# Attention over sequences of varied length: V projected by tiles of 512 columns, two runs of scores for two tiles, direct jumps between loop bodies

## Chip, cores, metric

One core of one Trainium2 chip. The metric is the device time of one execution in microseconds. Verdicts rest on ratios, which use fast runs alone; medians and ranges are of all runs of a kernel (among them one slow run each of e4, of e11 and of the kernel before). In the profile PE is TensorE, PEld its weight loads, DVE VectorE, ACT ScalarE, POOL GpSimd, SP SyncE; PEclk is the TensorE clock that was granted, in tenths of full speed (in the table by windows as a fraction).

## The reference

```python
# x: 32 x 512 x 512 fp32, w_qkv: 512 x 1536, lengths: 32 integers from 64 to 511, 8 heads of 64
for b in range(32):
    n = lengths[b]
    q, k, v = np.split(x[b, :n] @ w_qkv, 3, axis=-1)       # by heads: 8 x n x 64
    attn = softmax(q @ k.T / 8)
    output[b, :n] = attn @ v                                # the rows behind n stay zero
```

The lengths are data: the kernel sorts the sequences on the chip and picks the code for each pair at run time.

## The kernel before

The 32 sequences, sorted by length, form 16 pairs. A pair belongs to a *class* `k`, which computes N = 512 - 32k columns in T = ceil(N/128) tiles. Each class is one unrolled *body* with two halves. A half does the scores, exponentials and products of one sequence and projects Q, K and V of the next. For this input the pairs have the classes 0, 2, 4, 5, 5, 5, 6, 7, 8, 9, 9, 10, 11, 11, 12, 13. So there are two bodies of four tiles, six of three, six of two and two of one. Between bodies there are two steps by two classes (0 to 2 and 2 to 4), nine steps by one, and four repeats of the same class.

A half is a string of tokens, in the order of TensorE's work: `S` one run of scores with its exponential on ScalarE, `Q0`, `K0` a projection (*evicted*, that is copied out of the matmul's output bank, by VectorE, by ScalarE when lower case), `B0`/`b0` Q and K of a head pair together, `V0` a V group, `A0` attention times V with its normalization (`R`, `X` are its two VectorE parts when placed by hand), `O`, `P` the stores.

```python
    ORDER = {
        4: "S S Q0 A0 S S K0 V0 S S Q1 A1 S S K1 V1 S S Q2 A2 S S K2 V2 S S Q3 A3 S S K3 V3 O",
        3: "S S Q0 A0 K0 S S V0 Q1 A1 S S K1 V1 S S Q2 A2 K2 S S V2 Q3 A3 S S K3 V3 O",
        2: "S S V0 B0 A0 b1 A1 S V1 S B2 V2 O A2 A3 b3 P V3",
    }

    def vproj(pr, bank, h, i, T):          # the V of head pair i, for all T tiles
        ...                                # (T == 1: one group of 512 columns)
        for t in range(T):
            for c in range(NC):            # NC = 4
                mms.append(mm(pa[:, bank, t * P : (t + 1) * P],
                              xT[h][:, c, t * P : (t + 1) * P],            # stationary
                              w_r[:, c, 2 * D + i * P : 2 * D + (i + 1) * P],  # 128 moving columns
                              c == 0, c == NC - 1))
        group(... "dve" ... tensor_tensor(out=v_aug[...], in0=pa[...], in1=mask, op=ALU.mult))
```

The walk through the bodies is the same on every engine. The program stands in the order of the classes, and each body has a compare-and-branch at its head (skip it unless the class is this one) and one at its end (repeat it if the next pair has the same class). TensorE alone also gets a hint, some way into the first half, for the head branch of the next class (a mark ahead of a branch, tied to that branch, with a register as its condition):

```python
    def read_class(pr, h, N):              # after the third projection of the first half
        ...
                def hint(e):
                    cur, far = regs[e.engine][1], regs["far"]
                    e.reg_alu(far, cur, k + 2, ALU.is_lt)       # 1: class k+1 will not be skipped
                    ahead[k + 1] = e.mark_branch_hint_location(far)
                pr.add("pe", hint)

    def loops(e, name, body, pre1=None):
        r, cur = regs[e.engine]
        for k, N in enumerate(CLASSES):
            ...
            br = e.br_cmp(cur, k, lab, out_, "IS_EQ")           # else to out_, the head of k+1
            if name == "pe" and k in ahead:
                br.branch_hint(ahead[k])
            nc.switch_bb(lab, parent=top)
            body(e, N)
            e.br_cmp(cur, k, lab, out_, "IS_EQ")                # repeat
            nc.switch_bb(out_, parent=top)
```

The softmax here doesn't subtract the row's maximum and nothing guards it: scores larger than these inputs give would overflow.

## Time and profile before

| | before |
|---|---|
| time, median of four fast runs (range), those of the rounds with the kernel after | 369.78 us (368.31 to 371.26) |
| profiled span, mean granted clock | 367.7 us, 0.986 |
| TensorE busy | 349.1 us, 95% |
| start of the loop's first projection | 30.72 us |
| a half of four tiles, 512 columns | 19.50 us |
| two halves of three tiles, 352 columns | 25.6 us for both |

TensorE, busy 95% of the span, is the bound, so a change is read off the starts of its groups. Two further lines matter later. The first is the row of the granted clock in 40 slices of the span, the second the only entry for a pause without a visible cause ("issue") among TensorE's waits (columns: in total, times, longest).

```profile
PEclk9699999999999999999999999999999999999998
```

```profile
PE pa L219 <- issue: 0.4, 1, 0.4
```

Behind the start-up the clock drops only in the last slice, and no "issue" pause is longer than 0.4 us. That one stands at 109.69, inside a body, so none falls on the fifteen steps between bodies. (In the one-tile part, waits of up to 1.2 us are put down to TensorE's own sequencer, in the helper that waits for semaphores; their cause is not shown.)

### The profile page before, as it was taken

How to read it: one execution, taken by the hardware profiler on the slowest of the kernel's cores; microseconds unless marked ns; L12 is line 12 of the kernel's file. 1: busy time of each engine (PE TensorE's matmuls, PEld its weight loads, DVE VectorE, ACT ScalarE, POOL GpSimd, SP SyncE). 2: the span in 40 equal slices, each digit the busy share in tenths (PEclk: the TensorE clock that was granted, in tenths of full speed). 3: DMA queues.
4: the chain of work that ended last, by engine and by line, in shares of the span. 5: the costliest groups of instructions: out<-in, count | busy, mean ns of one | idle time of the engine just before them, and what ended most of it. 6: DMA issues, size and time to landing. Idle time of an engine off the chain costs nothing. (4 is left out here: it accounts for less than half of the span.)

```text
span 367.7 us, 12708 instructions
## 1 busy us (share of the span) xinstructions
PE 349.1 (95%) x4844; PEld 245.4 (67%) x4845; DVE 236.9 (64%) x537; ACT 229.2 (62%) x307; POOL 58.0 (16%) x85
## 2 busy tenths in 40 slices
PE   8699999999999999999999999999899999999882
PEld 3245566666656666666666677777789898887761
DVE  4455667666767667676766767676666666676562
ACT  5278778777776666666666757565566664654541
POOL 3062020202010110111011001110112112212120
PEclk9699999999999999999999999999999999999998
DMA  7969677458759677978759759969876566667673
GB/s 264 337 155 276 202 160 215 132 123 265 182 168 237 172 257 192 225 260 289 225 150 302 252 117 286 299 199 255 233 203 184 152 176 182 188 143 223 164 169 101
DMA packets 84582, 76.43 MB, mean 208 GB/s; under 512 B 42544, under 2 KB 63024, under 8 KB 84528
## 3 DMA queue, kind: packets, MB, share of 16 engines
q1 hardware_dynamic: 69376, 59.47, 59.8%
q10 hardware_dynamic: 15152, 16.26, 12.9%
q8 instruction: 32, 0.52, 0.6%
q14 instruction: 22, 0.18, 0.2%
HBM read 29.37 MB, written 36.70 MB: 180 GB/s over the span
## 5 line engine op out<-in xcount | busy, mean ns | idle before, releaser
L261 ACT ACTIVATE ep<-psc 128x704 f16<-128x704 f32 (+5 forms) x265 | 204.7, 821 | 101.3 <-PE psc L219 76.6
L219 PE MATMUL pa<-xT,w_r 128*128 128x352 f16 (+11 forms) x1056 | 161.6, 288 | 3.8 <-PEq L45 2.6
L291 DVE CAST qkT<-pa 128x352 f16<-128x352 f32 (+5 forms) x164 | 92.0, 561 | 59.5 <-PE pa L219 55.5
L219 PEld LDWEIGHTS pa<-xT,w_r 128*128 128x128 f16 x1056 | 81.4, 98 | 54.4 <-issue 27.9
L219 PE MATMUL pa<-w_r,xT 128*128 128x128 f16 (+1 forms) x1296 | 94.8, 221 | 0.1
L219 PEld LDWEIGHTS pa<-w_r,xT 128*128 128x128 f16 x1296 | 77.8, 98 | 18.4 <-issue 9.4
L324 DVE TENSOR_TENSOR v_aug<-pa,masks 128x384 f16<-128x384 f32 (+2 forms) x116 | 60.9, 525 | 31.5 <-PE pa L219 29.7
L219 PEld LDWEIGHTS pav<-v_aug,ep 128*128 128x128 f16 x1792 | 67.2, 98 | 11.7 <-ACT ep L261 3.5
L219 PE MATMUL pav<-v_aug,ep 128*128 128x65 f16 x1792 | 71.7, 194 | 2.5 <-ACT ep L261 2.4
L219 PE MATMUL psc<-qkT 64*128 64x352 f16 (+11 forms) x656 | 70.1, 299 | 1.4 <-PEq L45 0.9
L405 DVE SCALAR_TENSOR_TENSOR onat<-pav,masks,rcp 128x256 f32<-128x256 f32 (+2 forms) x128 | 51.9, 444 | 5.2 <-DVE rcp L381 0.7
L849 POOL CAST v_aug<-masks 128x24 f16 (+4 forms) x33 | 9.1, 276 | 282.1 <-POOLq L665 282.1
L844 POOL CAST x<-x_nat 128x1536 f16<-128x1536 f32 (+3 forms) x34 | 43.9, 1293 | 17.2 <-POOLq L665 16.2
L219 PEld LDWEIGHTS psc<-qkT 64*128 64x128 f16 x656 | 20.6, 94 | 21.5 <-issue 10.2
L289 ACT CAST qkT<-pa 128x448 f16<-128x448 f32 (+3 forms) x28 | 14.1, 504 | 24.4 <-ACTq L45 15.2
L381 DVE RECIPROCAL rcp<-pav 128x8 f32<-128x8 f32 (+1 forms) x68 | 14.7, 216 | 19.7 <-PE pav L219 16.0
L403 DVE TENSOR_TENSOR onat<-pav,rcp 128x512 f32<-128x512 f32 (+2 forms) x32 | 17.8, 557 | 1.1
L883 PE MATMUL psc<-zt 128*128 128x512 f16 x26 | 7.9, 468 | 1.7 <-DVE zt L905 1.7
L883 PEld LDWEIGHTS psc<-zt 128*128 128x128 f16 x26 | 2.8, 114 | 5.2 <-issue 1.9
L610 ACT ACTIVATE ep<-tiny 128x1024 f32<-128x1024 f32 x6 | 6.0, 1053 | 0.0
L790 ACT CAST w_r<-w_f 128x1024 f16<-128x1024 f32 x4 | 4.2, 1045 | 1.1 <-DMA w_f<-in_w_qkv_dram 1.1
L790 ACT ACT_TABLE_LOAD x1 | 1.3, 1283 | 3.2 <-issue 3.2
(48 smaller groups left out, 19.7 us busy)
## 6 DMA issues: line engine op xcount, KB each, us to landing
out_dram<-zt SPq DMA_DIRECT2D x16, 768.0 KB, 5.4
x_nat<-in_x_dram SPq DMA_DIRECT2D x12, 768.0 KB, 5.0
x_nat<-in_x_dram SPq DMA_DIRECT2D x8, 1024.0 KB, 6.6
out_dram<-onat ACTq DMA_DIRECT2D x28, 256.0 KB, 3.5
x_nat<-in_x_dram SPq DMA_DIRECT2D x12, 512.0 KB, 4.2
out_dram<-onat ACTq DMA_DIRECT2D x12, 384.0 KB, 3.9
out_dram<-onat SPq DMA_DIRECT2D x12, 384.0 KB, 3.6
out_dram<-zt SPq DMA_DIRECT2D x12, 256.0 KB, 4.6
```

The source lines that it names most:

```text
L219: return lambda e: e.matmul(o, lhsT, rhs, start=start, stop=stop)
L261: lambda e: e.activation(out=dst, in_=src, func=AF.Exp, scale=scale),
L289: group(pr, b, eng, mms, lambda e: e.copy(out=dst, in_=src))
L291: group(pr, b, eng, mms, lambda e: e.tensor_copy(out=dst, in_=src))
L324: lambda e: e.tensor_tensor(out=v_aug[h][:, 0:T, 2 * i : 2 * i + 2, 0:HD], in0=pa[:, bank, 0 : T * P].rearrange("p (t a d) -> p t a d", a= ...
L381: pr.add("dve", lambda e: e.reciprocal(out=rv, in_=den).then_inc(s_r, 1))
L403: ins = e.tensor_tensor(op=ALU.mult, **ops)
L405: ins = e.scalar_tensor_tensor(scalar=now[0][:, 1, t : t + 1], op0=ALU.mult, op1=ALU.mult, **ops)
L610: lambda e, a=a: e.activation(out=ep32[:, i + 1, a], func=AF.Copy, in_=tiny.unsqueeze(2).broadcast_to([P, NT, MAXS // 2]),).then_inc(s_ini ...
L844: e.tensor_copy(out=x16[h][:, 0:T, :], in_=x_nat[h][:, 0:T, :]).then_inc(s_xc[h], 1)
L849: e.tensor_copy(out=v_aug[h][:, 0:T, :, HD], in_=src[:, 0, 0:T].unsqueeze(2).broadcast_to([P, T, NH]),).then_inc(s_on[h], 1)
L883: e.matmul(psc[:, 1, 0, :], zt16[:, 0:P], zt16[:, 0:MAXS], start=True, stop=True)
```

## The change

It has four parts.

1. V by tiles for T = 3 and 4 and in the prologue (T = 1 had it already): the x tile stands still, all 512 V columns move, one group for each tile. T = 2 keeps the old form under the name `W`.
2. New orders: two runs of eight score matmuls for T = 2 instead of one of eight and two of four; some K and Q copies moved to ScalarE; V3 ahead of the last products, Q3 last.
3. Jumps: the end of a body compares the next class with its own, the next and the next but one, and jumps there directly.
4. Hints: TensorE, ScalarE and VectorE each get a hint for the jump to the body after next, and none for the next. The prologue and the bodies of classes 0 to 9 and 12 carry one; those of 10, 11 and 13 have no such jump.

The diff, cut to its core (cut: renamed variables, the halves rewritten for bodies of mixed classes, which `DOWN = 0` leaves unused, and a class table for 32 lengths):

```diff
-    def vproj(pr, bank, h, i, T):
+    def vproj(pr, bank, h, t):
+        mms = []
+        for c in range(NC):
+            mms.append(
+                mm(pa[:, bank, :], xT[h][:, c, t * P : (t + 1) * P], w_r[:, c, 2 * D : 3 * D],
+                   c == 0, c == NC - 1)
             )
+        group(
+            pr, f"a{bank}", "dve", mms,
+            lambda e: e.tensor_scalar(
+                out=v_aug[h][:, t, :, 0:HD],
+                in0=pa[:, bank].rearrange("p (h d) -> p h d", d=HD),
+                scalar1=now[0][:, 0, t : t + 1], scalar2=None, op0=ALU.mult,
+            ),
+        )
...
     ORDER = {
-        4: "S S Q0 A0 S S K0 V0 S S Q1 A1 S S K1 V1 S S Q2 A2 S S K2 V2 S S Q3 A3 S S K3 V3 O",
-        3: "S S Q0 A0 K0 S S V0 Q1 A1 S S K1 V1 S S Q2 A2 K2 S S V2 Q3 A3 S S K3 V3 O",
-        2: "S S V0 B0 A0 b1 A1 S V1 S B2 V2 O A2 A3 b3 P V3",
+        4: "S S Q0 A0 S S V0 k0 S S q1 A1 S S K1 V1 S S Q2 A2 R2 X2 S S K2 V2 S S V3 A3 O S S K3 Q3",
+        3: "S S k0 A0 Q0 S S V0 q1 A1 S S K1 V1 S S q2 A2 S S K2 V2 A3 R3 X3 S S K3 O Q3",
+        2: "S S W0 A0 B0 b1 A1 W1 S S B2 W2 A2 A3 R3 X3 O W3 P B3",
+        1: "Q k A0 V0 S O",
     }
...
-                def hint(e):
-                    cur, far = regs[e.engine][1], regs["far"]
-                    e.reg_alu(far, cur, k + 2, ALU.is_lt)
-                    ahead[k + 1] = e.mark_branch_hint_location(far)
+    def fetch(pr, at, to):                 # called with to = at + 2, after the fourth projection
+        if to not in targets(at) or to <= at + 1:
+            return
+        def fn(g, e):
+            e.reg_alu(regs[g], regs[e.engine][1], number(to), ALU.is_equal)
+            pr.ahead[g][to] = e.mark_branch_hint_location(regs[g])
+        for g in ("pe", "act", "dve"):
+            pr.add(g, lambda e, g=g: fn(g, e))
...
+        def leave(at, ahead):
+            for to in targets(at):         # itself, at + 1, at + 2
+                d = f"{name}_d{at}_{to}"
+                br = e.br_cmp(cur, number(to), f"{name}_b{to}", d, "IS_EQ")
+                if to in ahead:
+                    br.branch_hint(ahead[to])
+                nc.switch_bb(d, parent=top)
+            e.br(f"{name}_x{max(targets(at))}")
...
-            body(e, N)
-            e.br_cmp(cur, k, lab, out_, "IS_EQ")
+            leave(at, body(e, at) or {})
```

## The prediction

> **What bounds the kernel now.** I read the page's busy shares first, then the matmul timeline from start to start (recorded ends overlap the next start), then waits, then VectorE and ScalarE where TensorE waits.
>
> ```profile
> PE 349.1 (95%) x4844; PEld 245.4 (67%) x4845; DVE 236.9 (64%) x537; ACT 229.2 (62%) x307; POOL 58.0 (16%) x85
> ```
>
> TensorE is busy 95% of 367.7 us; no other engine is near. Of the missing 18.6 us most lies in the first 14 us and after 345 us. So what counts is the time from one group's start to the next group's start. Two pieces of its timeline, of a four-tile and a three-tile body (V is `pa<-w_r,xT`, Q and K are `pa<-xT,w_r`, scores `psc`):
>
> ```profile
> 32.67 0.61 PE L219 MATMUL psc<-qkT 64*128 64x512 f16 x4
> 33.21 1.04 PE L219 MATMUL pa<-xT,w_r 128*128 128x512 f16 x4
> 34.08 1.06 PE L219 MATMUL pa<-w_r,xT 128*128 128x128 f16 x16
> 35.07 0.61 PE L219 MATMUL psc<-qkT 64*128 64x512 f16 x4
> ...
> 115.66 0.84 PE L219 MATMUL pa<-w_r,xT 128*128 128x128 f16 x12
> 116.34 0.81 PE L219 MATMUL pa<-xT,w_r 128*128 128x384 f16 x4
> ```
>
> Four matmuls of 512 columns take 34.08 - 33.21 = 0.87 us, 0.2175 each. Twelve of 128 columns take 116.34 - 115.66 = 0.68, 0.0567 each. Sixteen take 0.99 where scores follow, of which 16 x 0.0567 = 0.91 is work and 0.08 is the step into the scores.
>
> The two-tile body, where runs of scores are of eight or four matmuls:
>
> ```profile
> 324.93 0.45 PE L219 MATMUL psc<-qkT 64*128 64x160 f16 x8
> 325.31 0.62 PE L219 MATMUL pa<-w_r,xT 128*128 128x128 f16 x8
> 325.77 0.72 PE L219 MATMUL pa<-xT,w_r 128*128 128x160 f16 x8
> ...
> 327.47 0.31 PE L219 MATMUL psc<-qkT 64*128 64x160 f16 x4
> 327.71 0.62 PE L219 MATMUL pa<-w_r,xT 128*128 128x128 f16 x8
> 328.26 0.31 PE L219 MATMUL psc<-qkT 64*128 64x160 f16 x4
> ```
>
> Eight together take 0.38; two fours take 2 x 0.24 or 0.25 = 0.49. The V group ahead takes 0.46 when a projection follows and 0.55 when scores follow. A run less saves 0.11 + 0.09 = 0.20 us.
>
> The waits of TensorE between 30 and 346 us, then the place where one arises, at the end of a three-tile body's second half (VectorE, then TensorE):
>
> ```profile
> PE pav L219 <- ACT ep L261: 2.4, 3, 1.1
> PEld pa L219 <- DVE qkT L291: 6.7, 22, 0.4
> ```
>
> ```profile
> 156.85 0.23 DVE L381 RECIPROCAL rcp<-pav 128x12 f32<-128x12 f32 x1
> 157.23 1.27 DVE L405 SCALAR_TENSOR_TENSOR onat<-pav,masks,rcp 128x256 f32<-128x256 f32 x3
> 158.41 0.51 DVE L291 CAST qkT<-pa 128x352 f16<-128x352 f32 x1
> ```
>
> ```profile
> 158.41 0.47 PE L219 MATMUL psc<-qkT 64*128 64x352 f16 x4
> 158.99 0.77 PE L219 MATMUL pa<-xT,w_r 128*128 128x352 f16 x4
> ```
>
> From the scores to the next projection are 0.58 us instead of the usual 0.40: the bank frees only when VectorE, after the A3 products, has copied K3 (158.92). Most of the 6.7 us of weight-load idle is ordinary lead; what TensorE really loses in the three-tile bodies is about 0.05 to 0.27 us at such places.
>
> [...]The trace shows no such gap on TensorE at the jump from class 0 to 2 (scores at 69.19, projection at 69.68: 0.49, as elsewhere in that body). [...]I take the 0.20 us from the trace.
>
> **The change, part by part.** The sixteen bodies, from the lengths: two of four tiles, six of three, six of two, two of one; each has two halves. `DOWN` is 0, so both halves keep one size and the "shorter" orders are never used.
>
> *V by tiles.* Four tiles: 4 groups of 0.907 become 4 of 0.870, 0.15 us a half, 4 halves: 0.6 us. Three tiles: 4 x 0.68 = 2.72 becomes 3 x 0.87 = 2.61, 0.11 a half, 12 halves: 1.4 us. The runs of scores stay eight and six. The eviction becomes tensor_scalar; the one-tile body has it at 749 ns for 128x512, against 4 x 558 or 4 x 694 now, so VectorE gains in three tiles and pays 0.2 us in four.
>
> *The prologue* also gets 512-column V, but its scores wait for ScalarE, which from 20.92 to 30.34 us does exponentials and memory fills without a gap. Nothing is gained. The class table doubles (32 x 15) and needs two more VectorE steps: about 1.2 us on VectorE before 10 us, mostly hidden by the input that lands at 11.84. Cost 0.2 us.
>
> *Evictions on ScalarE* (k0, q1, and q2 in three tiles). In four tiles ScalarE has 1.94 of each 2.4 us taken and gets two copies of 0.59 a half. By hand its lag grows to 0.5 us, just short of the slot that the next scores want. I count no wait.
>
> *Three-tile end of a half.* K3 is still copied after V2 and the A3 products, and k0 wants its bank. From A3's end to the wanted start: scores 0.41, K3 0.61, Q3 0.69, scores 0.41: 2.12 us (V3 gave 0.76 in place of 0.69). The products now also start behind the wider V2 eviction, about 0.1 later, so the bank is free at about 2.5 in a second half and 2.1 in a first. Waits of 0.25 to 0.6 instead of 0.12 to 0.27 at seconds, and 0 to 0.27 at firsts for the short classes: 1.5 us more over the bodies. The waits before q2 (about 0.5 us in all) go. Net cost 1.0 us; three tiles net -0.4 us.
>
> *Two tiles.* One run less: 12 x 0.20 = 2.4 us. But W3 moves ahead of B3, and its eviction waits behind A3's products. From A3's end (330.13) these are done at 331.69, W3 would be copied at 332.02: 1.9 us. W0 wants the bank after 0.46 + 0.64 + 0.38 = 1.48 at 160 columns, 1.8 at 224. That costs 0.2 to 0.5 us where columns are few, 0.8 in sum. Two body starts gain nothing, as ScalarE sets them (below): 0.4. The bridge to one tile waits for all banks, and its last one now frees 0.5 us later. Net -0.7 us.
>
> *Jumps.* An own or next class needs the same one or two compares as before; only a jump by two gets a new hint on ScalarE and VectorE, and this input has two such, both without a gap on TensorE. ScalarE does start late after a body, as here:
>
> ```profile
> 331.91 0.39 ACTq L673 DMA_DIRECT2D out_dram<-onat  x1
> 333.74 1.30 ACT L261 ACTIVATE ep<-psc 128x640 f16<-128x640 f32 x2 [2.34 <-issue]
> ```
>
> The 1.44 us from the end of the store's issue to the exponential cause one of the three waits of TensorE for `ep` (0.90 at 334.50). But this is a repeat of the same class, without a hint in either kernel. I count 0, give or take 1 us.
>
> Sum: +0.2 - 0.6 - 0.4 - 0.7 = -1.5 us, 367.9. The hand count charges every wait in full, and orders this particular look tried out; I shade to 367.6.
>
> **Rivals.** (1) All gain, no new wait: 0.6 + 1.4 + 2.4 us, and the present bank and ScalarE waits vanish too (about 3 us): 362 us. For it: the copies moved to ScalarE relieve VectorE. Against: K3 and W3 are still behind the products. (2) ScalarE becomes the bound in the four-tile bodies: 18 operations of 0.92 to 1.02 and 0.59 in 19.3 us is 91%; if the lag does not recover within a half, each of four halves loses up to 1 us: 371 us. Against: the run is 1.94 of 2.4 and 1.73 of 2.2 at 448. (3) Jumps stall VectorE, ScalarE or the DMA queue (now a taken jump, where the next body was run into): 0.5 us at fifteen bodies would be 375 us; the queues' idle time hides most of it. (4) The stretch before the two-tile bodies waits for zero stores (ScalarE 3.28 us at 257.9): a faster start only lengthens that wait.
>
> **Range.** All gain without waits gives 362, twice my waits 371. Range 363.8 to 371.0. Faster by over 2% needs less than 362.0, beyond the whole gain: 0.05. Slower by over 2% needs stalls at every body end: 0.04. Within: 0.91.
>
> **What would show it.** V groups of 16 and 12 matmuls at 0.87 to four, and halves of four tiles 0.15 us shorter; no gain before the loop. In three tiles, scores at a half's start followed by k0 after 0.6 to 0.8 us with a wait for VectorE; in two tiles, two score runs a half and a wait ahead of W0 in the 160-column bodies; the bridge's idle of 0.86 at 1.3. I am wrong if those waits are absent (then 364 to 365), if ScalarE delays scores in four tiles, or if gaps with the sequencer as releaser stand at body ends.

The sum: +0.2 (start) - 0.6 (four tiles) - 0.4 (three tiles) - 0.7 (two tiles) = -1.5 us, and 0 for the jumps. In rival (3), the 0.5 us a body is a supposition from no trace, and that idle time hides most of it was the author's estimate (the page before leaves VectorE idle for 36% and ScalarE for 38% of the span), which the result did not bear out.

## The result and the profile after

| | before | after |
|---|---|---|
| median of four fast runs (range) | 369.78 us (368.31 to 371.26) | 396.32 us (393.34 to 397.11) |
| profiled span, clock | 367.7 us, 0.986 | 395.3 us, 0.956 |

The ratio is 1.070 (95% interval 1.063 to 1.078): the change makes the kernel 7% slower. (A ratio here and below is the mean time of one kernel's fast runs over that of the other's fast runs of the same rounds, so not quite the ratio of the medians.)

The page of the kernel after, busy shares and granted clock:

```profile
PE 355.8 (90%) x4172; PEld 220.9 (56%) x4173; DVE 221.8 (56%) x495; ACT 239.5 (61%) x339; POOL 58.5 (15%) x85
```

```profile
PEclk9699999999989989999999899999999999979995
```

TensorE has 672 matmuls less, yet is busy 6.7 us longer, over a span 27.6 us longer. The clock row says why it is busy longer: it now has dips in the middle of the run. And TensorE's waits say where the rest is (columns as before):

```profile
PE pav L228 <- issue: 6.3, 3, 2.8
PE pa L228 <- issue: 5.4, 3, 3.0
PE pa L228 <- DVE v_aug L335: 4.1, 3, 3.6
PE psc L228 <- issue: 3.5, 2, 1.9
```

"issue" is 6.3 + 5.4 + 3.5 = 15.2 us in eight pauses, where it was 0.4 us in one. The engine waited for nothing that the profile shows. To find where, set the start of each body's first scores beside the same start before. The lag (after minus before) rises at some steps and not at others:

| body of class | 0 | 2 | 4 | 5 | 5 again | 5 again | 6 | 7 | 8 | 9 | 11 | 11 again | end |
|---|---|---|---|---|---|---|---|---|---|---|---|---|---|
| lag at its first scores, us | 0.1 | 1.6 | 4.5 | 5.4 | 9.7 | 9.8 | 9.8 | 14.3 | 14.5 | 16.7 | 17.9 | 23.9 | 27.6 |

(For class 0 it is taken at the first projection, 30.85 against 30.72, as the scores ahead of it are split in one of the two.) A pause falls before a body's first scores or up to 8 us behind them, and then shows at the next entry: the 4.3 us between 5 and its repeat belong to the step from 4 to 5, the 4.5 between 6 and 7 to the step from 5 to 6. The repeats of class 5 themselves cost next to nothing (the lag goes from 9.7 to 9.8 us). TensorE's timeline at the step from class 4 to class 5 (start, duration, group; in brackets the idle time before it and what ended it):

```profile
141.97 0.76 PE L228 MATMUL pa<-xT,w_r 128*128 128x352 f16 x4
142.57 0.28 PE L228 MATMUL pav<-v_aug,ep 128*128 128x65 f16 x4
145.44 0.92 PE L228 MATMUL pav<-v_aug,ep 128*128 128x65 f16 x14 [2.58 <-issue]
...
146.99 1.35 PE L228 MATMUL pa<-xT,w_r 128*128 128x352 f16 x4
```

A run of 18 products is cut after four, stands for 2.58 us, and goes on. Nothing in the program separates the fourth product from the fifth. In the kernel before, the same products in the same body are one run:

```profile
136.86 0.71 PE L219 MATMUL pav<-v_aug,ep 128*128 128x65 f16 x18
137.51 0.47 PE L219 MATMUL psc<-qkT 64*128 64x352 f16 x4
```

And the price goes on afterwards: the projection of four matmuls takes 0.60 us from start to start at 141.97 and 148.13 - 146.99 = 1.14 us behind the pause. The same place by windows (window, its length, busy us and instructions of PE, PEld, DVE, ACT, POOL, then granted clock, DMA share, GB/s):

```profile
137.00:142.60 5.60, 5.46 (x52) 2.93 (x50) 3.04 (x7) 4.47 (x7) 1.76 (x2) 1.00 0.65 230
142.60:145.40 2.80, 0.25 (x5) 0.13 (x3) 0.44 (x1) 0.45 (x1) 0.00 (x0) 1.00 0.46 78
145.40:149.00 3.60, 3.56 (x25) 1.81 (x26) 1.84 (x4) 1.41 (x2) 0.00 (x0) 0.53 0.26 55
```

All engines are nearly idle in the pause (the others soon have nothing left from TensorE), then the granted clock is 0.53 for 3.6 us: 3.6 x 0.47 = 1.7 us more. So a stall of 2.6 us costs 4.3, which is the step of the lag from 5.4 to 9.7.

Not only TensorE stalls. VectorE in the first body of class 11, then TensorE:

```profile
346.26 0.21 DVE L392 RECIPROCAL rcp<-pav 128x8 f32<-128x8 f32 x1 [0.31 <-PE pav L228]
350.05 0.88 DVE L416 SCALAR_TENSOR_TENSOR onat<-pav,masks,rcp 128x256 f32<-128x256 f32 x2 [3.58 <-issue]
```

```profile
351.32 1.03 PE L228 MATMUL pa<-w_r,xT 128*128 128x128 f16 x8 [3.60 <-DVE v_aug L335]
```

Read alone, the last line says "W waits for the V eviction", which would be an effect of the new order. VectorE's line shows that VectorE itself stood 3.58 us for nothing visible between a reciprocal and the multiplication with its result. It is again a pause with no visible cause, handed on. But it stands 10 us into the body, and neither this body nor the one before carries a hint, so what sets it off is not shown. TensorE waits for VectorE at this place in e2 and e6 too (2.28 and 3.52 us), and nowhere for this copy longer than 0.4 us in e3 and e5 below.

The sum of the whole difference, as an estimate from these views: 15.2 us of "issue" pauses, less 0.4 before, and 4.1 us behind VectorE are 18.9. The clock lost 395.3 x 0.044 = 17.4 us against 367.7 x 0.014 = 5.1, 12.3 more; counted only where TensorE is busy behind 14 us (by windows of 1.5 us) it is 12.1 against 2.3, some 10 more. Other waits grew by some 2 us (for the exponential 3.5 against 2.4, for the K3 copy 1.6 against 0.2, less 0.4 at the sequencer). Together about 31, less 2 to 3 us of gains of the orders (below): about 28, where 27.6 are to be explained.

The parts that the prediction worked out by groups are there. The wide V in a four-tile body, four matmuls in 34.20 - 33.33 = 0.87 us:

```profile
33.33 1.04 PE L228 MATMUL pa<-w_r,xT 128*128 128x512 f16 x4
34.20 1.03 PE L228 MATMUL pa<-xT,w_r 128*128 128x512 f16 x4
```

And the wait at the start of a three-tile body, behind the K3 copy:

```profile
168.10 0.53 PE L228 MATMUL psc<-qkT 64*128 64x352 f16 x4
168.87 0.77 PE L228 MATMUL pa<-xT,w_r 128*128 128x352 f16 x4 [0.23 <-DVE qkT L300]
```

### The profile page after: what moved, and what is told of

It reads as the page before. It is cut to its first block, busy times and chain, and to the rows that moved or that the text cites. A ratio compares the mean times of both kernels' runs of the same rounds, so it can differ in the third digit from the quotient of the medians.

```text
span 395.3 us, 11465 instructions
## 1 busy us (share of the span) xinstructions
PE 355.8 (90%) x4172; PEld 220.9 (56%) x4173; DVE 221.8 (56%) x495; ACT 239.5 (61%) x339; POOL 58.5 (15%) x85
## 3 DMA queue, kind: packets, MB, share of 16 engines
q10 hardware_dynamic: 15152, 16.26, 12.1%
## 5 line engine op out<-in xcount | busy, mean ns | idle before, releaser
L300 DVE CAST qkT<-pa 128x512 f16<-128x512 f32 (+5 forms) x132 | 74.0, 569 | 82.2 <-PE pa L228 76.7
L228 PEld LDWEIGHTS pa<-xT,w_r 128*128 128x128 f16 x1056 | 85.1, 100 | 60.7 <-issue 26.5
L228 PE MATMUL pav<-v_aug,ep 128*128 128x65 f16 x1792 | 74.0, 196 | 10.0 <-issue 6.3
L228 PEld LDWEIGHTS pav<-v_aug,ep 128*128 128x128 f16 x1792 | 68.8, 99 | 21.2 <-issue 6.7
L228 PEld LDWEIGHTS pa<-w_r,xT 128*128 128x128 f16 x624 | 45.2, 100 | 38.7 <-issue 12.3
L312 DVE TENSOR_SCALAR v_aug<-pa,masks 128x512 f16<-128x512 f32 x60 | 45.2, 753 | 29.1 <-PE pa L228 27.4
L228 PEld LDWEIGHTS psc<-qkT 64*128 64x128 f16 x656 | 22.9, 95 | 38.1 <-issue 30.2
L298 ACT CAST qkT<-pa 128x352 f16<-128x352 f32 (+5 forms) x60 | 28.8, 480 | 16.8 <-ACTq L52 13.0
L335 DVE TENSOR_TENSOR v_aug<-pa,masks 128x256 f16<-128x256 f32 x48 | 20.2, 421 | 8.8 <-PE pa L228 8.5
L414 DVE TENSOR_TENSOR onat<-pav,rcp 128x512 f32<-128x512 f32 (+2 forms) x32 | 17.9, 558 | 1.1
```

The costliest lines, as they stand in the source:

```text
L228: return lambda e: e.matmul(o, lhsT, rhs, start=start, stop=stop)
L298: group(pr, b, eng, mms, lambda e: e.copy(out=dst, in_=src))
L300: group(pr, b, eng, mms, lambda e: e.tensor_copy(out=dst, in_=src))
L312: lambda e: e.tensor_scalar(out=v_aug[h][:, t, :, 0:HD], in0=pa[:, bank].rearrange("p (h d) -> p h d", d=HD), scalar1=now[0][:, 0, t : t + ...
L335: lambda e: e.tensor_tensor(out=v_aug[h][:, 0:T, 2 * i : 2 * i + 2, 0:HD], in0=pa[:, bank, 0 : T * P].rearrange("p (t a d) -> p t a d", a= ...
L414: ins = e.tensor_tensor(op=ALU.mult, **ops)
```

## The experiments

The trace says *that* engines stood with no visible wait, not which part of the change makes them do so. Theory J: leaving by jumps, with their hints, makes them stand. Its rivals: the new orders are slow by themselves (O), or the mere place of the code, which the change shifts everywhere, is the cause (P). Within J, the jump itself (J1) stands against the hints (J2). Twelve kernels were run, and all gave right results. In what follows "before" is that kernel in the same rounds: 371.12 us for the first four runs, 371.57 for the next four, 369.99 for the three after those, and 369.28 for the last. Times of different rounds are set side by side only for differences of many us. Each trace is of one execution. Five medians lie outside every range set beforehand (e1, e2, e7, e10, e11), mostly by little; the expectations are printed with each run, less some words on mechanisms that no run shows (the cuts are marked).

### e1: the orders of the kernel after with the walk of the kernel before

The kernel after, with `leave` and the hints taken out, and the compare at a body's head and end and the single TensorE hint put back.

```diff
-            e.reg_alu(regs[g], regs[e.engine][1], number(to), ALU.is_equal)
-            pr.ahead[g][to] = e.mark_branch_hint_location(regs[g])
-        for g in ("pe", "act", "dve"):
+            e.reg_alu(regs["pe"], cur, number(to), ALU.is_lt)      # TensorE alone
+            hints[at + 1] = e.mark_branch_hint_location(regs["pe"])
...
-            leave(at, body(e, at) or {})
+            body(e, at)
+            e.br_cmp(cur, number(at), lab, out_, "IS_EQ")
```

> The changed kernel with only the way between bodies put back: one compare per class in the order of the classes, one hint on TensorE, as in the kernel before. Theory 'jumps' (the pauses of 1 to 3.6 us with releaser 'issue' come from the jumps at the end of a body): 364 to 370 us, no 'issue' pause above 0.5 us on TensorE, granted clock back at 0.98 or more. Rival 'orders'[...]: 388 us or more.

Measured: 375.65 us (373.46 to 377.36), ratio 1.015 (1.010 to 1.020), clock 0.982. Of a loss of 26.5 us 4.5 are left, so J holds for most of it; but the orders are not the gain of 1.5 us that was predicted, they cost these 4.5. Part of that is again a pause: one of 2.04 us "issue" at the step from 2 to 4, with the clock at 0.67 over the 4.2 us behind it (1.4 us more). All other "issue" pauses of the kernel after are gone.

### e2: the kernel before with the jumps and hints of the kernel after

```diff
-            body(e, N)
-            e.br_cmp(cur, k, lab, out_, "IS_EQ")
+            leave(at, body(e, CLASSES[at]) or {})      # leave() as in the change
...
-                    e.reg_alu(far, cur, k + 2, ALU.is_lt)
+            e.reg_alu(regs[g], regs[e.engine][1], to, ALU.is_equal)   # to = at + 2, on three engines
```

> The kernel before with only the jumps and their hints (+2, on TensorE, ScalarE, VectorE); V, orders and evictions as before. Theory 'jumps': 390 to 400 us with the same pauses after the steps 0->2, 2->4, 4->5, 5->6. Rival 'orders': 368 to 373 us.

Measured: 405.07 us (401.62 to 406.88), ratio 1.091 (1.082 to 1.099). The jumps with their hints alone, on unchanged orders, cost more than the whole change. TensorE pauses at the same steps: 3.43 us at 0 to 2, 3.23 at 2 to 4, 2.74 at 4 to 5, 1.42 at 5 to 6, and more behind (the longest, 3.73, at 7 to 8). O falls as the main cause.

### e3: the kernel after without its hints

```diff
     def fetch(pr, at, to):
-        if to not in targets(at) or to <= at + 1:
-            return
+        return
```

> The changed kernel with the hints taken out, jumps kept. If the hint itself does the harm[...]: 370 to 382 us, pauses gone at the steps by one class. If the jump does it[...]: 394 to 402 us, pauses at the steps by one class unchanged, those by two the same or longer.

Measured: 379.34 us (375.61 to 381.16), ratio 1.021 (1.012 to 1.030). Taking away the *hints*, with every jump kept, gives back 17 of the 26.5 us. TensorE at the step from 4 to 5, for which the kernel after was shown above:

```profile
142.08 0.71 PE L228 MATMUL pav<-v_aug,ep 128*128 128x65 f16 x18
142.72 0.47 PE L228 MATMUL psc<-qkT 64*128 64x352 f16 x4
```

The 18 products are one run, and no "issue" pause is left at any step by one (the one-tile part keeps a wait of 1.55 us that is put down to the sequencer, where the longest was 1.17 in the kernel before). So a jump to the next body shows no such pause here without hints, and with them five of the nine such steps show one (0.68 to 2.96 us in the kernel after). Pauses are left at the two steps by two: 2.17 and a further 0.83 us at 0 to 2, 1.78 us at 2 to 4. (ScalarE's wait for zero stores before the two-tile part also grew, to a 4.07 us wait of TensorE for the exponential. The prediction names this place in rival (4).)

### e4: the kernel after with a hint for the next body as well

If the pauses at the steps by one come from the next body having no hint of its own, a second hint should take them away.

```diff
-        if to not in targets(at) or to <= at + 1:
+        if to not in targets(at) or to <= at:
...
+                        fetch(pr, at, at + 1)
                         fetch(pr, at, at + 2)
```

> The changed kernel with a hint for the next class as well. If the pauses at the steps by one class come from a missing hint: 372 to 384 us (the pauses at 145, 224, 282, 299 us gone). If a hint can't cover a jump of this kind: within 4 us of 396.

Measured: 395.98 us (393.00 to 401.49), ratio of its fast runs 1.065 (1.059 to 1.072): no change. Its profiled run was a slow one, so its trace is not used. The second hint with the same condition does not help. Either a hint for the next body is not the point, or the condition works the other way round than assumed. The next two runs take up the second.

### e5 and e6: the condition inverted, and the condition constant 0

The kernel after sets the register to 1 when the jump will be taken. e5 sets it to 1 when it will *not* be taken, and e6 sets it to 0 always.

```diff
# e5
-            e.reg_alu(regs[g], regs[e.engine][1], number(to), ALU.is_equal)
+            e.reg_alu(regs[g], regs[e.engine][1], number(to), ALU.not_equal)
# e6
+            e.reg_mov(regs[g], 0)
```

> The changed kernel with the hint's condition turned round: 1 where the next class is not the one hinted. e3 showed that the hints cost about 17 us, and in e4 a second hint did not help. [...]Rival 'the condition counts, but in the opposite sense': 370 to 380 us, with no pause at the steps by one class and none, or short ones, at 0->2 and 2->4.

> The changed kernel with the hint's condition fixed at 0, never to be jumped. If 0 switches a hint off: 376 to 382 us as without hints (e3). [...]If the sense is opposite: 390 us or more, with pauses at the repeats of a class too.

(The theory set against the rival in e5, that the condition makes no difference, was put at within 5 us of 396 there and at 390 to 400 us in e6.)

Measured: e5 378.76 us (376.75 to 382.28), ratio 1.019 (1.012 to 1.026); e6 399.32 us (398.08 to 400.75), ratio 1.078 (1.071 to 1.085). TensorE at the step from 0 to 2, in the kernel after and then in e5:

```profile
67.28 1.90 PE L228 MATMUL pa<-xT,w_r 128*128 128x512 f16 x8
70.75 0.55 PE L228 MATMUL psc<-qkT 64*128 64x448 f16 x4 [1.57 <-issue]
```

```profile
67.08 1.90 PE L228 MATMUL pa<-xT,w_r 128*128 128x512 f16 x8
68.92 0.55 PE L228 MATMUL psc<-qkT 64*128 64x448 f16 x4
```

With 0 in the register at this step by two the pause is gone in e5, and in e6 TensorE has no "issue" pause there either (68.64 to 69.13 from the scores to the projection; but VectorE stood 3.51 us at 73.06, and TensorE waited 1.14 us for its copy; up to there the registers of e5 and e6 differ only for the hint of the prologue). Seven of the nine steps by one start from a body with a hint (4 to 9 and 12). In e5, where the register is 1 there, TensorE has no "issue" pause behind any of them; where it is 0, in e6 as in the kernel after, it has one behind five (not behind 6 to 7 and 9 to 10). The step from 4 to 5 in e6:

```profile
145.44 0.28 PE L228 MATMUL pav<-v_aug,ep 128*128 128x65 f16 x4
...
148.49 0.95 PE L228 MATMUL pav<-v_aug,ep 128*128 128x65 f16 x14 [2.76 <-issue]
```

It is the same cut after the fourth product, so e6, where no register is ever 1, is as bad as the kernel after. (Its expectation added pauses at the repeats of a class, should the sense be opposite: there are none.) What was measured is this: **at the step from 0 to 2, whose hinted jump is taken, TensorE paused 1.57 us with 1 in the register (the kernel after) and not with 0 (e5, e6). At the seven hinted steps by one, whose hinted jump is not taken, it paused behind five with 0 (the kernel after, e6) and behind none with 1 (e5).** So where the values made a difference on TensorE, the better one was 0 for a jump that was taken and 1 for one that was not. The kernel after has the other value at all nine steps (396.3 us), e5 this one (378.8 us), and e6 0 throughout (399.3 us). In the kernel before, where another branch carries the hint, `cur < k+2` is 0 at the two steps by two, whose head branch skips, and 1 at the nine by one, and no pause falls on any of them. That the register's value matters is shown by e5 and e6; what a hint sets off, and why a wrong one costs time, is not shown by any view. Two things don't fit those values. At the step from 2 to 4 TensorE pauses 2.05 us in e5 and 2.06 in e6, with 0, as in the kernel after with 1 (1.92). And in the body of class 4 TensorE waits 3.35 us in e5 (at 132.97) behind VectorE, which stood 3.77 us for nothing visible between a reciprocal and its multiplication; e6 has the same pause, 3.69 us. The kernel after, with 1, and e3, without hints, don't have it. So on VectorE a 0 ahead of a jump that is taken went with a pause of 3.7 us, twice.

### e7: the wide V alone

The kernel before with wide V for three and four tiles and in the prologue, and the least change of order that it needs. A first build with the orders untouched was found to race: nothing put V3's eviction ahead of the next half's first products, which now need every tile of V. So wide V forces a part of the new orders, V3 (V2) ahead of the last products.

```diff
-        4: "... S S Q3 A3 S S K3 V3 O",
-        3: "... S S V2 Q3 A3 S S K3 V3 O",
+        4: "... S S V3 A3 S S K3 Q3 O",
+        3: "... S S V2 A3 S S K3 Q3 O",
```

> The kernel before with V by tiles of 512 columns for three and four tiles and in the first stage, with the smallest change of order that is free of races (V3 before A3 and Q3 last in four tiles, V2 before A3 and K3, Q3 last in three); its walk from class to class, evictions of Q and K on VectorE and two-tile body are those of before. My forecast's terms: halves of four tiles 0.15 us shorter, of three tiles 0 to 0.1 shorter; 368 to 371 us. If wide V brings waits of its own: 373 us or more.

Measured: 371.51 us (371.11 to 374.75), ratio 1.004 (0.996 to 1.012). No jump was changed, and still a pause stands at the step from 2 to 4:

```profile
103.46 1.69 PE L219 MATMUL pa<-xT,w_r 128*128 128x448 f16 x8
107.37 0.50 PE L219 MATMUL psc<-qkT 64*128 64x384 f16 x4 [2.23 <-issue]
```

Where nothing disturbs them the halves show what V is worth. A 448-column half goes from 18.22 to 18.10 us. The three bodies of class 5 (pairs of 352-column halves) go together from 76.93 to 76.86 us, 25.6 each in both: three wide groups are shorter than four narrow ones (3 x 0.87 = 2.61 us against 4 x 0.68 = 2.72), and the wait for the K3 copy (1.7 us in six waits over the run, where 0.2 in one was) takes it back.

### e10: the same, with the old code in two bodies that never run

Is the pause at 2 to 4 the doing of V or of the place of the code? e10 is e7 with narrow V and the old order in the bodies of 480 and 416 columns (classes 1 and 3). No pair of this input has these classes. What runs is e7 instruction for instruction; only the code that is jumped over is longer, as before.

```diff
+        narrow = N in (480, 416)
+        toks = (OLD4 if narrow else ORDER[T]).split()
```

> e7 (wide V alone) with narrow V put back in the bodies of classes 480 and 416, which never run with these lengths: the instructions carried out are those of e7, only the code skipped over is longer. e7 and e1 pause for 2.0 to 2.2 us at the step 2->4, which the kernel before does not. If that pause is a matter of where the code lies: gone or moved, and 2 to 4 us less than e7 (367 to 369.5). If wide V itself makes it: as e7, 371 to 372.

Measured: 369.90 us (368.49 to 370.49), ratio 1.000 (0.996 to 1.005), and the pause is gone:

```profile
103.09 1.69 PE L219 MATMUL pa<-xT,w_r 128*128 128x448 f16 x8
104.71 0.52 PE L219 MATMUL psc<-qkT 64*128 64x384 f16 x4
```

So P is real, as a second cause: here, with longer code that never runs, the pause of 2.23 us behind the step over it was gone. And wide V shows no gain: without the pause it is at 1.000, with an interval that a gain of 1 us (0.27%) would still fit in.

### e8 and e9: two runs of scores alone

e8 is the kernel before with the two-tile order of the change (without moving `R3 X3`), e9 the smallest edit that saves the run and keeps the old tail.

```diff
-        2: "S S V0 B0 A0 b1 A1 S V1 S B2 V2 O A2 A3 b3 P V3",
+        2: "S S V0 A0 B0 b1 A1 V1 S S B2 V2 A2 A3 O V3 P B3",      # e8
+        2: "S S V0 B0 A0 b1 A1 V1 S S B2 V2 O A2 A3 b3 P V3",      # e9
```

> The kernel before with only the two-tile order of the changed kernel (two runs of scores a half). My forecast's terms: undisturbed halves 0.20 us shorter at 224 and 256 columns, waits ahead of W0 in the short ones, bridge 0.4 later; 367 to 370.5 us. If the order makes new waits larger than that: 372 us or more.

> A candidate to beat both: the kernel before, with V1 moved ahead of the scores in the two-tile order so that they come in two runs, and the tail of a half (b3 on ScalarE, V3 last) kept as it was. From e8: the gain of 0.2 us per undisturbed half stays, the waits ahead of W0 (0.17 to 0.39 us) and the 0.4 us more at the bridge go: 1.5 to 2.5 us less than before in the profile, ratio 0.993 to 0.997. If the ratio is 0.999 or more, the gain is lost to a wait elsewhere (ScalarE at the start of the bodies).

Measured: e8 369.60 us (369.20 to 369.96), ratio 0.997 (0.990 to 1.003); e9 368.56 us (367.84 to 370.75), ratio 0.997 (0.993 to 1.001). The run of eight in e9:

```profile
292.44 0.61 PE L219 MATMUL pa<-w_r,xT 128*128 128x128 f16 x8
292.99 0.56 PE L219 MATMUL psc<-qkT 64*128 64x224 f16 x8
```

Undisturbed two-tile halves go from 7.98, 7.24, 7.38 and 6.96 us to 7.77, 7.02, 7.17 and 6.80: 0.21, 0.22, 0.21 and 0.16 less, where 0.20 was worked out. In e8 the waits for the V eviction ahead of the first V group (four, 1.0 us in all) are as predicted; e9, whose last group is V3 again, has two of 0.3 us in all. By its mean neither order gains more than 1.5 us, and neither interval excludes none.

### e11: jumps without hints on the kernel before

e2 without its hints, to set J1 against J2 on the old orders.

```diff
# e2 with:
     def fetch(pr, at, to):
+        return
```

> The kernel before with the jumps but no hint at all. If e2's loss is the hints' (as e3 and e5 say): 371 to 376 us, with pauses at most at the two steps by two classes. If the jumps themselves do it in this kernel: 385 us or more.

Measured: 377.83 us (375.31 to 384.61), ratio 1.016 (1.011 to 1.020). TensorE pauses 3.02 us at 0 to 2 and 2.86 us at 2 to 4, and another 3.01 us in the one-tile part is put down to the sequencer; at the steps by one there is none. So the jumps cost about 6 us (0.016 of 370) and the hints the rest of e2's 34: some 27 us (1.0905 over 1.0156 is 1.074).

One more thing stands in this trace. The pause of 3.02 us, longer than the one shown at the step from 4 to 5, leaves the clock alone (columns as above):

```profile
68.20:71.25 3.05, 0.04 (x3) 0.01 (x2) 0.69 (x1) 0.03 (x1) 0.00 (x0) 1.00 0.86 290
71.25:79.25 8.00, 8.00 (x112) 4.93 (x113) 4.59 (x10) 5.91 (x7) 2.19 (x2) 1.00 0.46 65
```

The pause of 2.86 us at 2 to 4 is followed by 0.52 over the next 2 us in the same run (from the scores to the projection 0.74 us, where 0.43 at 114.59), and in e3 the clock stays at 1.00 behind 2.17 us. So in these runs the length of a pause alone did not decide whether the clock dropped.

### e12: the best of the parts

e10 and e9 together: wide V with the old code in the unused bodies, and two runs of scores with the old tail. The edits are those shown.

> The candidate from e9 and e10 together: walk, evictions and hint of the kernel before, wide V (narrow in the two bodies that never run, as in e10) and two runs of scores with the old tail (e9). If the two add: ratio 0.992 to 0.997, 366 to 369 us, no pause with releaser 'issue' above 0.5 us. If the code's new place brings a pause back: 370 us or more.

Measured: 367.88 us (367.06 to 369.08), ratio 0.997 (0.994 to 1.000), no "issue" pause among TensorE's waits. It is the best version made here, level with e9, and its interval just reaches 1.0003. The gain over the kernel before is not shown.

## Why the prediction was wrong, point by point

- **The step that failed: "Jumps ... I count 0, give or take 1 us."** Jumps and hints together cost some 20 us on the new orders (the ratio goes from 1.015 in e1 to 1.070) and 34 on the old (e2). Two errors lie in it. First, "a jump by two gets a new hint" counted hints by the jumps that are taken. But the instruction is executed in the bodies of classes 0 to 9 and 12 whichever jump follows, and most of its effect falls behind steps by *one*, where e6 and the kernel after stall and e3 and e5 don't. Second, I took from the trace before that a jump by two needs no help ("no such gap on TensorE at the jump from class 0 to 2"). That was under the old walk, with a hint whose register was 0 there. With jumps and no hint TensorE pauses 2.17 us (e3) to 3.02 us (e11) at this step. A gap that is absent under one walk and hint was read as a gap that cannot come.
- **The rival set aside.** Rival (3), jumps that stall, was named with gaps that have "the sequencer as releaser" and priced at 375, by 0.5 us a body, with a chance of 0.04 for more than 2%. The stalls are of up to 3.7 us on TensorE (e2, from 7 to 8) and sit at few steps, and their releaser reads "issue". Why it was dropped, "the queues' idle time hides most of it", looked at the wrong engine: TensorE itself stands, 15.2 us in eight pauses, and, busy 95% of the span before, it has next to nothing behind which to hide them. The rival was overruled by one gap-free jump.
- **The price of a stall was not in any rival.** The granted clock dropped behind five of the nine pauses of the kernel after (the eight of "issue" and the one behind VectorE), to 0.50 to 0.66 over about 4 us: 0.66 behind 1.92 us, 0.53 behind 2.58, 0.57 behind 2.76, 0.50 behind the 3.60 us wait for VectorE and behind 2.96. Behind the other four, of 0.68 to 1.74 us, it was 1.00 over the next 2 us. Over the run this is about 10 us of the 27.6. No one length parts the two: the clock was 0.67 behind 2.04 us in e1 and 1.00 behind 3.02 us in e11.
- **V by tiles.** The group times were right (0.87; halves of four tiles 0.12 us shorter at 448 columns, 0.15 predicted), and so was the wait for K3's copy (1.6 us in the kernel after where 0.2 was, 1.5 more predicted). "Three tiles net -0.4 us" was nearer 0: the three bodies of class 5 take 76.93 us before, 76.86 in e7 and 77.03 in e1. In sum e10 stands at 1.000. Two steps of the working were off by little: 12 halves at 0.11 us are 1.3 us and not 1.4, and VectorE doesn't gain in three tiles, since 3 x 749 ns is 2.25 us where 4 x 558 was 2.23. (The forecast's 367.9 counts from 369.42, the median of three runs of the kernel before that was known then.)
- **Two tiles.** -0.20 a half was right (e9: 0.16 to 0.22), and so were the waits ahead of W0 (0.2 to 0.4 us) and the bridge, 0.86 predicted to become 1.3 and measured at 1.26.
- **Start.** +0.2 was predicted; the loop's first projection comes 0.13 us late in the kernel after (30.85 against 30.72) and 0.57 in e1, with the same code before it but for one hint, so this term varies by more than its size. The 1.2 us on VectorE was right: its masks end 1.20 us later (at 10.96 against 9.76).
- **The orders as a whole: -1.5 us was predicted, +4.5 measured (e1).** Missing are the pause at 2 to 4 (2.0 us and 1.4 of clock; e7 against e10 shows a pause at the same step that goes with the length of unused code, and for e1 this was not run) and a longer wait for the zero stores. That wait of TensorE in e1 is 2.4 us where it was 1.1. Rival (4) had the place, but as a limit to a gain, not as a loss.
- **ScalarE in four tiles** did not become the bound: these halves are shorter, as written. Nor did the "all gain" rival come true.

What stays open. What a hint sets off was not shown, and how its cost divides among the three engines that carry hints was not separated. Why the repeats of class 5 never pause was not tested. Why the step from 2 to 4 pauses in e5 and e6 (2.05 and 2.06 us), with the value that was better at 0 to 2, is not settled: in e7 longer unused code takes the pause away (e10), and e5 with such a filler was not run. The pauses of VectorE inside a body (3.77 us in e5, 3.69 in e6, 3.58 in the kernel after) are unexplained, and so are the sequencer's wait in the one-tile part and what besides its length makes the clock drop behind a pause.

## What to carry to other kernels

A pause with the releaser "issue" in the middle of a straight run of matmuls went away here without any change to the matmuls, when the hints were taken out (e3: none left at the steps by one): look at which branch and which hint came before it, and test by taking hints and jumps out one at a time. Before a control-flow change is priced at zero because the old trace shows no gap, ask whether the change takes away something that stands there: here the old walk with its hint had no gap from 0 to 2, and jumps without hints had 2.17 (e3) and 3.02 us (e11). And a stall of two or three microseconds on TensorE cost nearly double here (2.6 us became 4.3), where the granted clock was 0.53 behind it; behind one of 3.02 us it was 1.00 (e11), so read the clock there.
